# The planner's rate for gathers beside a dense expert stage: 380 in place of 360

## The chip, the cores and the metric

The kernel runs on one core of a Trainium2 chip. The metric is device time in microseconds, the median of several executions. The profile is of one execution.

## The reference

The reference is one residual block on 1024 tokens of width 1024 in float32. Three token mixers (stick-breaking attention, dilated window attention, attention into 256 memory tokens) share one normalised input, are gated, summed and projected, and added to x. Then comes the part that matters here, an expert mixer. Each token gets 8 heads x 16 = 128 of 16384 experts, each expert being one row of u and one of v:

```
act = gelu(einsum('chkd,cd->chk', u[ic], hc))     # ic: 128 chosen experts per token
w   = gate * act
out = einsum('chk,chkd->cd', w, v[ic])
```

## The kernel before, in words

The 1024 tokens are eight tiles of 128. The front (mixers, gating, output projection, and the choice of the experts) takes the tiles in three groups of 2, 3 and 3. The expert mixer is done in two ways.

**By gather**, for six tiles (0, 1, 2, 3, 5, 7). A tile takes 128 steps (class `Experts`, `step`, L1133). A step covers one expert for each of 128 token-head slots: GpSimd gathers 128 rows of u and later 128 rows of v with an indirect DMA each (`fetch`, L1097). VectorE multiplies the u rows with the spread tokens `hb` and sums them (L1151). After each fourth step ScalarE and VectorE make gelu and weights, and TensorE adds the v rows of those four steps into `po` (L1177, eight matmul instructions per step in the profile). There are `UP, VP = 5, 6` buffers for u and v rows. Every 32 steps a quarter of the output rows is loaded (`row`, L1142), added to and stored.

**Densely**, for the tiles 4 and 6 (`DENSE`, ND = 2), by `dense()`: all 16384 experts, in 128 blocks e of 128. A block has a product of u with the tokens (`product`, L1297 to L1305: 24 matmuls of 256 columns with high and low parts `uh`, `ul`, `hh`, `hl`), a gelu, a weighting by the gate matrix `g` (`weigh`, L1337), and 12 matmuls of 512 columns that sum into the output (`wh`, `wl` by `vh`, `vl`). The weights `ur` and `vr` come in pairs of blocks, 1 MB a load, through SP's queue (`load`, L247), with two buffers each; a `g` load of 1 MB serves eight blocks. ScalarE and VectorE split each weight block into high and low parts (L128, L1275). Before that the last tile's gate matrix is built (L1316: 80 fills) and stored to `gd`, and 22 blocks (`RUN`) get an early product at full precision. The products of the other 106 blocks follow, each with the sums of the block that is 22 earlier; the last 22 blocks have sums alone.

The order of the two is set when the program is built, by a planner (L1424 on). It keeps two sums: `pe`, the planned time of TensorE, and `dma`, that of the transfers, and places one gather step after another. Ahead of each it takes dense or front work from a generator in small pieces (`fill`, L1412), for as long as planned DMA is ahead of planned TensorE or TensorE is behind `due`:

```
L1416    spent = (cost[0] - c + 50) * slow[0], (moved[0] - m) / bw[0]
...
L1428    due = max(due + LEAST, pe - LEAST)
L1429    while filler[0] is not None and (dma > pe or pe < due):
L1430        a, b = fill(1)
L1431        pe += a
L1432        dma += b
L1433    pe += TOKEN_NS
L1434    dma += TOKEN_BYTES / bw[0]
```

Costs come from the code itself: a matmul through `mm` costs 4 x (columns/2.4 + 2.5) ns, one through `mmr` columns/2.4 + 3 ns, a gate fill 800 ns, and each fill 50 ns on top. `load` counts its bytes (L245). `slow` and `bw` have two values each: 1.38 and 295 bytes per ns during the front, and from L1405, where the front is closed and `dense()` begins, `SLOW[1]` = 1.1 and `BW[1]`. A step counts `TOKEN_NS` = 700 ns and `TOKEN_BYTES` = 128 x 8192 + 3 x 8192 = 1,073,152 bytes; `LEAST` is 3000 ns. When the generator has run out, the gather steps that are left follow alone.

Of the kernel before, what the change touches and what calls it, by code (L numbers as in the profile page):

```python
# [34 lines left out]
RUN = 22  # L35


BW = 295.0, 360.0
SLOW = 1.38, 1.1
TOKEN_NS, TOKEN_BYTES = 700.0, 128 * 8192 + 3 * 8192.0  # L40
LEAST = 3000.0
# [36 lines left out]
def block_kernel(ctx: ExitStack, tc: tile.TileContext, io):  # L78
# [1309 lines left out]
    def rest():  # L1388
        n0 = built = 0
        odd = False  # L1390
        for g in range(len(GROUPS)):
            for stage in phase1(g, n0, GROUPS[g], ready):
                if stage and built < ND:

                    want = sum(n < n0 for n in DENSE)
                    while len(stored) < want:
                        sides(1)
                    odd = not odd
                    for _ in range(999 if stage == 2 else 1 + odd):
                        if built < want:  # L1400
                            built = next(gates)
                yield
            n0 += GROUPS[g]
        front.close()
        slow[0], bw[0] = SLOW[1], BW[1]  # L1405
        yield from dense()

    filler = [rest()]
    slow, bw = [SLOW[0]], [BW[0]]
    pe = dma = due = 0.0  # L1410
# [86 lines left out]
```

## Time and profile before

| | us |
|---|---|
| median of 3 runs | 3561.07 |
| lowest and highest run | 3557.21, 3573.94 |
| the profiled execution, its own time | 3568.14 |
| its span, first to last instruction | 3566.4 |
| PE, DVE, POOL, ACT busy | 3196.1, 2341.1, 1778.4, 1353.6 |
| mean DMA rate over the span | 332 GB/s |

PE is TensorE's matmuls, PEld its weight loads, DVE is VectorE, ACT ScalarE, POOL GpSimd, SP the queue of SyncE that issues most loads. In the windows view each row is a stretch of the span; for each engine it has the busy microseconds and, in brackets, the number of instructions, then the granted TensorE clock, the mean busy share of the 16 DMA engines, and the rate. With a tile's name the busy times are of the instructions on that tile alone, but clock, share and rate are still those of the whole core. Rows of the waits view have who waited, for whom, the total in us, the number of times and the longest. Rows of a tile's view have minimum, median and maximum duration in ns and the first and last start in us.

### The profile page before, as it was taken

What the parts mean: (1) busy time and instruction counts of PE and PEld (TensorE: products, weight loads), DVE (VectorE), ACT (ScalarE), POOL (GpSimd) and SP (SyncE); (2) the same over time, 40 slices, a digit from 0 to 9 for tenths busy, and PEclk for the clock granted to TensorE, in tenths of its full rate; (3) what the DMA queues carried; (4) which work ended last, traced back from release to release, by engine and by line L of the source; (5) the groups of instructions that cost most, each with busy time, mean ns of one, the idle gap of its engine ahead of it and who ended that gap; (6) DMA issues with size and microseconds to landing.
All of it is one profiled execution on the core that took longest, in us unless ns stands there. A gap on an engine that the chain in (4) does not pass through costs nothing.

```text
span 3566.4 us, 60764 instructions
## 1 busy us (share of the span) xinstructions
PE 3196.1 (90%) x22802; PEld 2361.1 (66%) x22802; DVE 2341.1 (66%) x5985; ACT 1353.6 (38%) x2729; POOL 1778.4 (50%) x1544
## 2 busy tenths in 40 slices
PE   6999989989999889999998999776779999999954
PEld 6889856656555766666565657654568888888710
DVE  5444487565545468996656665798867677777654
ACT  4443135554411214656544222222324444444410
POOL 0000036656566556666555655566745444544476
PEclk9989989999999999999999999897899999999965
DMA  4425669999899999999998999989999999999999
GB/s 151 139 84 182 206 221 334 333 348 331 313 406 392 403 363 347 337 331 350 331 355 296 391 391 400 350 325 348 393 386 393 365 382 384 394 379 372 344 383 362
DMA packets 346430, 1185.54 MB, mean 332 GB/s; under 512 B 38744, under 2 KB 80216, under 8 KB 326680
## 3 DMA queue, kind: packets, MB, share of 16 engines
q0 software_dynamic: 221184, 805.40, 59.6%
q1 hardware_dynamic: 102672, 337.95, 26.0%
q10 hardware_dynamic: 22280, 38.31, 2.8%
q8 instruction: 180, 2.95, 0.3%
q14 instruction: 114, 0.93, 0.1%
HBM read 1142.18 MB, written 39.32 MB: 331 GB/s over the span
## 4 chain that ended last, share of the span: by engine, by line
PE 61%; DMA 15%; DVE 13%; issue 5%; ACT 3%; POOL 2%; ACTq 0%; SPq 0%; POOLq 0%; DVEq 0%
PE bank L117 32%; PE bank L1195 20%; PE po L1177 7%; DMA u<-in_u,iT 7%; DVE u L1151 3%; DMA v<-in_v,iT 3%; PE pb L1090 1%; DMA b3d<-sp 1%; PE bank L121 1%; POOL v L1097 1%; POOL u L1097 1%; DMA g<-gd 1%; ACT L126 1%; DMA gd<-g 1%; ACT e L128 1%
## 5 line engine op out<-in xcount | busy, mean ns | idle before, releaser
L1097 POOL DMA_INDIRECT u<-in_u,iT x768 | 916.2, 1193 | 956.1 <-DVE i L865 489.6
L1097 POOL DMA_INDIRECT v<-in_v,iT x768 | 861.4, 1122 | 818.8 <-PE po L1177 646.0
L1151 DVE SCALAR_TENSOR_TENSOR u<-u,hb 128x1024 f32<-128x1024 f32 x768 | 926.7, 1222 | 440.1 <-ACT hb L128 256.3
L1177 PE MATMUL po<-v,wz 128*32 128x256 f32 x6144 | 444.8, 416 | 155.3 <-DMA v<-in_v,iT 88.6
L117 PE MATMUL bank<-wide,w 128*128 128x384 f32 x1536 | 519.6, 492 | 1.8 <-DMA w<-in_w_gate 1.8
L1177 PEld LDWEIGHTS po<-v,wz 128*32 128x32 f32 x6144 | 182.0, 115 | 375.0 <-DMA v<-in_v,iT 119.0
L117 PEld LDWEIGHTS bank<-wide,w 128*128 128x128 f32 x1536 | 292.3, 192 | 201.3 <-issue 6.8
L128 ACT ACTIVATE hb<-pb 128x512 f32<-128x512 f32 x384 | 208.2, 594 | 397.2 <-PE pb L1090 251.3
L117 PEld LDWEIGHTS bank<-w,wide 128*128 128x128 f32 x2304 | 263.0, 192 | 7.4 <-issue 2.2
L117 PE MATMUL bank<-w,wide 128*128 128x128 f32 x2304 | 265.3, 275 | 0.2 <-DMA w<-in_w_out 0.2
L1195 PE MATMUL bank<-hh,ul 128*128 128x256 f32 x848 | 240.0, 283 | 1.2 <-DVE ul L1275 1.2
L1195 PE MATMUL bank<-hh,uh 128*128 128x256 f32 x848 | 240.9, 284 | 0.0
L1195 PE MATMUL bank<-hl,uh 128*128 128x256 f32 x848 | 239.9, 283 | 0.0
L117 PE MATMUL bank<-big,w 128*128 128x256 f32 (+1 forms) x1280 | 235.6, 341 | 1.2 <-DMA w<-in_w_pq 1.2
L117 PEld LDWEIGHTS bank<-big,w 128*128 128x128 f32 x1280 | 208.3, 193 | 27.0 <-issue 3.0
L128 ACT ACTIVATE e<-bank 128x512 f32<-128x512 f32 (+2 forms) x208 | 109.6, 527 | 306.8 <-PE bank L117 301.2
L1195 PE MATMUL bank<-vh,wh 128*128 128x512 f32 x512 | 202.9, 403 | 3.1 <-ACT vh L128 3.1
L1195 PE MATMUL bank<-vl,wh 128*128 128x512 f32 x512 | 201.9, 394 | 2.1 <-DVE vl L1275 2.0
L1195 PE MATMUL bank<-vh,wl 128*128 128x512 f32 x512 | 199.4, 389 | 0.0
L126 ACT ACT_TABLE_LOAD x144 | 184.8, 1283 | 21.7 <-issue 8.8
L128 ACT ACTIVATE w<-bank 128x256 f32<-128x256 f32 x128 | 49.3, 385 | 366.9 <-PE bank L1195 285.5
L1275 DVE TENSOR_TENSOR vl<-vr,vh 128x1024 fp32r<-128x1024 f32 x128 | 156.9, 1226 | 32.7 <-ACT vh L128 32.7
(297 smaller groups left out, 5659.9 us busy)
## 6 DMA issues: line engine op xcount, KB each, us to landing
ur<-in_uT SPq DMA_DIRECT2D x64, 1024.0 KB
vr<-in_vd SPq DMA_DIRECT2D x64, 1024.0 KB
w<-in_w_in SPq DMA_DIRECT2D x102, 512.0 KB
w<-in_w_gate SPq DMA_DIRECT2D x72, 512.0 KB
w<-in_w_pq SPq DMA_DIRECT2D x48, 512.0 KB
g<-gd SPq DMA_DIRECT2D x16, 1024.0 KB
w<-in_w_o SPq DMA_DIRECT2D x48, 256.0 KB
w<-in_w_out SPq DMA_DIRECT2D x24, 512.0 KB
```

The lines of the kernel that those rows point to most:

```text
L117: nc.tensor.matmul(out, lhsT, rhs, **kw)
L121: nc.tensor.transpose(out, in_, ident)
L126: nc.scalar.preload_act_table_set(s)
L128: nc.scalar.activation(out, in_, f, **kw)
L1090: nc.tensor.matmul(pb, which[:, jj].rearrange("p q s -> p (q s)"), box["b3"][:, f], start=True, stop=True)
L1097: nc.gpsimd.indirect_dma_start(out=t, out_offset=None, in_=io[kind], in_offset=bass.IndirectOffsetOnAxis(ap=ap, axis=0))
L1151: nc.vector.scalar_tensor_tensor(u, u, 1.0, self.hb, op0=OP.mult, op1=OP.mult, accum_out=self.parts[:, i:i + 1])
L1177: nc.tensor.matmul(po[32 * k:32 * k + 32, h:h + 256], wz[:, i, :], v[:, 256 * k:256 * k + 256], start=jj == 0 and i == 0, stop=jj == QB - ...
L1195: nc.tensor.matmul(out, lhsT, rhs, **kw)
L1275: nc.vector.tensor_sub(lo, r[:, x], hi)
```

## The change

One constant of the planner changes, the second of the two rates. It is used in L1405 alone, and from there in L1416 and L1434.

```
-BW = 295.0, 360.0
+BW = 295.0, 380.0
 SLOW = 1.38, 1.1
 TOKEN_NS, TOKEN_BYTES = 700.0, 128 * 8192 + 3 * 8192.0
 LEAST = 3000.0
```

No instruction is added or taken away. The order in which dense pieces and gather steps are issued can differ from the place where the front is closed.

More of the change, by code (lines that the diff above doesn't have):

```diff
@@ L35 @@
 RUN = 22
-BW = 295.0, 360.0
+BW = 295.0, 380.0
 SLOW = 1.38, 1.1
```

## The prediction

> **What bounds the kernel now.** I read the page first, then windows cut at the stage borders, the waits of each stage, and the chain that ended last.
>
> ```profile
> span 3566.4 us, 60764 instructions
> DMA  4425669999899999999998999989999999999999
> GB/s 151 139 84 182 206 221 334 333 348 331 313 406 392 403 363 347 337 331 350 331 355 296 391 391 400 350 325 348 393 386 393 365 382 384 394 379 372 344 383 362
> q0 software_dynamic: 221184, 805.40, 59.6%
> L1097 POOL DMA_INDIRECT u<-in_u,iT x768 | 916.2, 1193 | 956.1 <-DVE i L865 489.6
> L1097 POOL DMA_INDIRECT v<-in_v,iT x768 | 861.4, 1122 | 818.8 <-PE po L1177 646.0
> ur<-in_uT SPq DMA_DIRECT2D x64, 1024.0 KB
> vr<-in_vd SPq DMA_DIRECT2D x64, 1024.0 KB
> g<-gd SPq DMA_DIRECT2D x16, 1024.0 KB
> ```
>
> The page gives the sizes. The 1536 gathers moved 805.4 MB, 0.524 MB each, so a gather step (one u, one v) moves 1.049 MB. The rate of 360 acts only once the front is closed, so only the end of the span can change. It has four stages, whose borders are the first and last product (hl,uh) and the last sum (vh,wl):
>
> ```profile
> L1195 PE MATMUL bank<-hl,uh x848: 279/283/283, 2653.3 to 3320.8; 128*128 128x256 f32 x170
> L1195 PE MATMUL bank<-vh,wl x512: 387/389/402, 2656.4 to 3400.7; 128*128 128x512 f32 x171
> ```
>
> ```profile
> core 0: us, PE busy (x) PEld busy (x) DVE busy (x) ACT busy (x) POOL busy (x), PEclk, DMA share, GB/s
> 2380.00:2653.30 273.30, 184.39 (x1250) 125.78 (x1250) 222.40 (x727) 72.10 (x216) 162.64 (x135) 0.83 0.95 362
> 2653.30:3320.80 667.50, 666.99 (x4895) 575.13 (x4895) 478.41 (x741) 309.90 (x514) 319.11 (x244) 1.00 0.99 380
> 3320.80:3400.70 79.90, 75.27 (x415) 54.91 (x413) 54.62 (x87) 34.06 (x56) 38.27 (x32) 1.00 0.90 336
> 3400.70:3566.40 165.70, 78.35 (x542) 16.24 (x540) 82.07 (x156) 17.59 (x46) 117.80 (x115) 0.54 0.97 380
> ```
>
> I call them prelude, body, end and tail. In the body PE is busy 666.99 of 667.50 us while DMA also shows a share of 0.99. The waits say which of the two is the limit. These are the body's only waits for DMA; then the two largest of SP's queue there; then the tail's three largest for DMA:
>
> ```profile
> DVE u L1151 <- DMA u<-in_u,iT: 2.9, 1, 2.9
> POOL v L1097 <- DMA u<-in_u,iT: 0.3, 1, 0.3
> ```
>
> ```profile
> SPq L247 <- DVE ul L1275: 212.7, 40, 8.8
> SPq L247 <- DVE vl L1275: 202.9, 48, 7.3
> ```
>
> ```profile
> PEld po L1177 <- DMA v<-in_v,iT: 90.9, 41, 3.3
> PE po L1177 <- DMA v<-in_v,iT: 66.9, 50, 2.4
> DVE u L1151 <- DMA u<-in_u,iT: 65.1, 51, 4.5
> ```
>
> In the body nobody waits for data (2.9 us in 667.5), and the dense loads wait for a free buffer, not for DMA. PE sets the pace. In the tail it is the reverse: PE and DVE wait for each gather. So work on DMA that leaves the tail and fits beside the body's matmuls is gained, less what it costs PE there.
>
> **How many steps move.** The planner adds 0.7 us of planned time and 1,073,152 bytes per step, and fills with dense work while planned DMA is ahead. Over a stage with P us of planned dense work and D bytes of dense transfers it therefore places n = (P - D/rate) / (1,073,152/rate - 0.7) steps. The divisor is 2.281 us at 360 and 2.124 us at 380.
>
> One product of the body is 24 matmuls of 109.7 ns, 12 of 216.3 ns and three fills of 50 ns, times 1.1: 5.916 us; its bytes are 1.049 MB of weights and an eighth of a g load, 1.180 MB. That gives 1.157 steps at 360 and 1.324 at 380, so for 106 products 122.6 and 140.3: 17 to 18 more. The prelude has 14 waiting fills (22.4 us), 80 gate fills (68.0 and, for 64 of them, two matmuls, 28.6), 22 early products (76.9) and 0.3 for six fills: 196.1 times 1.1 is 215.7 us. Its bytes are 24 MB-sized transfers (13 ur, 8 stores to gd, the tokens, one vr, one g), 25.2 MB. n goes from 63.9 to 70.4, 7 more. The end has 46 pieces of six sums (1.348 us each, times 1.1: 68.2 us) and 12 such transfers, 12.6 MB; it goes from 14.6 to 16.5, 2 more. I take 7, 17 and 2: 26 steps leave the tail. The trace bears out the formula at 360, eight po matmuls to a step:
>
> ```profile
> 2653.30:3320.80 667.50, 58.66 (x968) 28.28 (x968) 1.68 (x4) 1.00 0.99 380
> 3320.80:3400.70 79.90, 7.74 (x128) 3.75 (x128) 0.42 (x1) 1.00 0.90 336
> ```
>
> ```profile
> 3400.70:3566.40 165.70, 0.00 (x0) 0.00 (x0) 73.88 (x120) 0.00 (x0) 56.53 (x55) 0.54 0.97 380
> ```
>
> The body has 968/8 = 121 steps, the end 16. The last row is of tile u, with two DVE records to a step: 60 steps lie in the tail, so 34 would be left.
>
> **The tail, minus 67.6 us.** Two price rows, the tail's undisturbed stretch and a short full stretch of the body:
>
> ```profile
> 2640.00:2700.00 60.00, 58.84 (x382) 49.55 (x381) 44.49 (x77) 25.77 (x44) 26.16 (x21) 0.96 1.03 398
> 3420.00:3480.00 60.00, 28.70 (x192) 5.27 (x192) 30.58 (x56) 4.92 (x13) 45.99 (x47) 0.50 1.03 409
> ```
>
> At 409 GB/s a step takes 2.56 us; the whole tail, with its lead-in and drain, 165.7/60 = 2.76. Lead-in and drain stay, so I take 2.6, near the first: 26 x 2.6 = 67.6, bounds 66.6 and 71.8.
>
> **The body, plus 21.** What a step costs PE is seen in the chain, where four steps' po matmuls lie between two dense pieces:
>
> ```profile
> 3100.94 22.48 PE bank L1195 x144
> 3123.43 1.86 PE po L1177 x32
> 3125.83 21.09 PE bank L1195 x138
> ```
>
> From 3123.43 to 3125.83 are 2.40 us, 0.60 per step. 17 steps add 10.2 us: by PE the body is 677.7 us. By DMA it has 667.5 x 380 GB/s = 253.7 MB and 17.8 MB more, 271.5 MB: 664 us at 409, 682 at 398, 714 at 380. So both limits come out nearly equal, and where they do each sometimes waits for the other. The cover is the dense loads' second buffer and eleven gather buffers; if it is gone, PE waits for ul or vl behind a late load. I take 688.5, 10.8 over the PE bound, which asks for 394 GB/s, near the 398 of the full stretch. Bounds: +10 and +47 (380 GB/s is all there is).
>
> **The prelude, plus 13.** Its last 210 us are nearly full already:
>
> ```profile
> 2440.00:2520.00 80.00, 67.53 (x467) 49.77 (x468) 64.13 (x235) 25.53 (x84) 51.79 (x41) 0.94 0.99 384
> 2520.00:2610.00 90.00, 69.96 (x451) 47.27 (x451) 80.96 (x267) 25.32 (x90) 60.25 (x51) 0.89 1.00 391
> ```
>
> Seven steps bring 7.3 MB. Beside the 210 x 388 = 81.5 MB there they end 6 us later if DMA reaches 409, 19 later at 388. I take 13, between.
>
> **The end, plus 2.** Here PE is idle for 79.90 less 75.27, 4.6 us, into which two steps of 0.60 fit. Against it stands 2 x 2.6 = 5.2 if each delays a load by its own transfer. Bounds 0 and 5; I take 2.
>
> A count may also shift by one step per stage. POOL's queue is passed by 26 pairs of gathers earlier than before; it is busy 319 of 667.5 us in the body. SP's queue gets the row loads (L1142, four per 32 steps) of 26 steps sooner, three or four of them, with dense loads queued behind; the second buffer covers those. Nothing is added or removed in bytes, matmuls or splits.
>
> Sum: 13 + 21 + 2 - 67.6 = -31.6 us. The span goes from 3566.4 to 3534.8, the profiled execution's own 3568.1 to 3536.5. That execution lies 7 us above the median of the runs, 3561.1, from which the forecast is 3529.5.
>
> **The rivals.** Full gain: the body takes its steps at PE's price. For it: nobody waits for data now. 6 + 10 + 0 - 71.8 = -56, 3505. Chance 0.17.
>
> No change, because DMA is already at its limit: each step costs in the body what it cost in the tail. For it: the share of 0.99 and the 380 GB/s of both body and tail. Against: 398 and 409 in shorter stretches. 47 + 19 + 5 - 67.6 = +3, 3564. With what lies between, 0.22. The Trainium skill has a rule for this side: "DMA: Bandwidth & Descriptors", Specifications, sets the HBM limit per core at about 358 GB/s. By it a plan at 380 asks for what can't be had: the 27.3 MB of the 26 steps would take 76 us where they go, against 68 saved, +8 in all by this estimate. This case's trace disagrees: the body's 380 and the tail's 409 lie above that limit. "HBM Reference", Specifications (TRN2), says that a core streaming alone measures about 425, which these rows come nearer to.
>
> Slower: with the queues full, a dense load lands after its use, PE stalls at ul or vl, buffers come free late, SP's next load is issued late, and DMA idles, as in the end, where DMA fell to 336 GB/s:
>
> ```profile
> ACT vh L128 <- DMA vr<-in_vd: 5.9, 2, 3.0
> ```
>
> At 358, midway between 380 and 336, the body takes 758 us, +91, and the sum is 91 + 19 + 5 - 67.6 = +47, 3608. It makes the kernel slower by over 0.5% only from a body of 730 us, below 372 GB/s. Against it: 11 gathers stay in flight whether PE stalls or not. 0.06.
>
> No effect: the planner's other condition, 3.0 us of planned time per step, sets the count. Against: in the body a step comes every 667.5/121 = 5.5 us. 0.02, at 3561.
>
> **How the numbers follow.** The forecast's chance is 0.53. What a measurement can tell from no change is about 0.5%, 17.8 us. Forecast and full gain are faster by more (0.70); no change and no effect lie within (0.24); 0.06 is slower. The range goes from just under the full gain, 3502, to 3558, near no change: above it are the slower case and part of the no-change case, below it almost nothing.
>
> **What would show it.** In the profile after, the first product comes at about 2666 instead of 2653, and the body from first to last product takes about 688 us with some 138 steps. The tail has 34 steps (68 records on u) and is near 98 us. The body's GB/s rises to about 394, with short waits for ul, vl or u new in it. The forecast is wrong if the body's rate stays near 380 and the body grows by 40 us or more, or if the tail still holds 60 steps.

## The result, and the profile after

The changed kernel takes 3549.23 us (median of 6 runs, 3540.80 to 3550.15), the kernel before, beside it, 3571.22 (6 runs, 3557.21 to 3574.48). The ratio is 0.9942, 95% interval 0.9921 to 0.9963: 0.58% faster, where the forecast was 0.9% (31.6 of 3568.1 us). Run once more on another chip, the ratio was 0.9931 (0.9908 to 0.9954). The profiled execution after has its own time of 3549.34 us and a span of 3547.6, that is 18.8 us less than the span before, not 31.6.

The page after:

```profile
span 3547.6 us, 60760 instructions
DMA  4425669899899999999998999998999999999999
GB/s 152 140 86 179 208 219 344 329 347 327 313 406 401 405 367 337 336 339 342 343 342 283 388 400 399 348 341 332 361 380 383 405 393 396 401 396 406 372 352 369
```

The DMA digits say the same as before, 9 almost everywhere, but in the 32nd to 37th slice, all body, the rate is 393 to 406, where it was 365 to 394. Next the rows that give the stage borders, then the windows cut there (PE, PEld, DVE, ACT, POOL busy, then clock, DMA share, GB/s), then the same windows for tile po, and the tail for tile u:

```profile
L1195 PE MATMUL bank<-hl,uh x848: 278/283/415, 2680.0 to 3367.2; 128*128 128x256 f32 x170
L1195 PE MATMUL bank<-vh,wl x512: 387/389/632, 2684.5 to 3450.0; 128*128 128x512 f32 x171
```

```profile
2380.00:2680.00 300.00, 195.79 (x1294) 129.12 (x1293) 234.08 (x745) 73.93 (x218) 169.14 (x148) 0.81 0.94 355
2680.00:3367.20 687.20, 681.68 (x5052) 582.32 (x5052) 495.08 (x779) 315.06 (x527) 357.64 (x278) 0.99 1.01 394
3367.20:3450.00 82.80, 77.40 (x415) 55.95 (x413) 56.40 (x92) 35.12 (x58) 42.68 (x35) 0.98 0.94 357
3450.00:3547.60 97.60, 47.77 (x338) 10.19 (x336) 46.98 (x90) 9.74 (x25) 65.64 (x64) 0.53 0.93 365
```

```profile
2680.00:3367.20 687.20, 67.69 (x1120) 32.81 (x1120) 2.11 (x5) 0.99 1.01 394
3367.20:3450.00 82.80, 7.74 (x128) 3.75 (x128) 0.00 (x0) 0.98 0.94 357
```

```profile
3450.00:3547.60 97.60, 0.00 (x0) 0.00 (x0) 40.64 (x66) 0.00 (x0) 31.27 (x30) 0.53 0.93 365
```

The body has 1120/8 = 140 steps instead of 121, the end 16 as before, the tail 66/2 = 33 instead of 60. Set against the forecast, stage by stage:

| stage | before, us | after, us | change | forecast (bounds) |
|---|---|---|---|---|
| prelude, to the first product | 273.3 | 300.0 | +26.7 | +13 (6 to 19) |
| body | 667.5 | 687.2 | +19.7 | +21 (10 to 47) |
| end | 79.9 | 82.8 | +2.9 | +2 (0 to 5) |
| tail | 165.7 | 97.6 | -68.1 | -67.6 |

Three of the four terms came within 1.3 us, and together 0.9 us below their sum. The prelude took 13.7 us more than its term and 7.7 more than its upper bound; that is the miss of 12.8. In the body there are now waits for transfers and split weights that were absent or shorter before (DVE's for u was 2.9), each of them short, as said. Four of the largest:

```profile
DVE u L1151 <- DMA u<-in_u,iT: 27.0, 13, 3.2
ACT vh L128 <- DMA vr<-in_vd: 7.4, 3, 3.7
PEld bank L1195 <- DVE vl L1275: 6.6, 5, 3.1
PE bank L1195 <- DVE vl L1275: 5.0, 3, 2.8
```

### The profile page after: what moved, and what is told of

The parts are those of the page before. It is cut to its first block, busy times and chain, and to the rows that moved or that the text cites. A ratio compares the mean times of both kernels' runs of the same rounds, so it can differ in the third digit from the quotient of the medians.

```text
span 3547.6 us, 60760 instructions
## 1 busy us (share of the span) xinstructions
PE 3194.0 (90%) x22802; PEld 2366.4 (67%) x22802; DVE 2337.2 (66%) x5985; ACT 1354.3 (38%) x2729; POOL 1768.6 (50%) x1544
## 4 chain that ended last, share of the span: by engine, by line
PE 60%; DMA 15%; DVE 14%; issue 5%; ACT 4%; POOL 2%; ACTq 1%; SPq 0%; POOLq 0%; DVEq 0%
PE bank L117 33%; PE bank L1195 17%; PE po L1177 7%; DMA u<-in_u,iT 5%; DVE u L1151 4%; DMA v<-in_v,iT 3%; DMA b3d<-sp 2%; PE pb L1090 1%; PE bank L121 1%; DMA gd<-g 1%; DMA vr<-in_vd 1%; POOL v L1097 1%; POOL u L1097 1%; ACT L126 1%; DMA ur<-in_uT 1%
## 5 line engine op out<-in xcount | busy, mean ns | idle before, releaser
L1097 POOL DMA_INDIRECT v<-in_v,iT x768 | 842.4, 1097 | 764.1 <-PE po L1177 595.1
L1177 PE MATMUL po<-v,wz 128*32 128x256 f32 x6144 | 434.8, 411 | 112.1 <-DVE wz L1166 54.3
L1195 PE MATMUL bank<-hh,ul 128*128 128x256 f32 x848 | 240.8, 284 | 0.4 <-DVE ul L1275 0.4
```

The lines of the kernel that those rows point to most:

```text
L1097: nc.gpsimd.indirect_dma_start(out=t, out_offset=None, in_=io[kind], in_offset=bass.IndirectOffsetOnAxis(ap=ap, axis=0))
L1177: nc.tensor.matmul(po[32 * k:32 * k + 32, h:h + 256], wz[:, i, :], v[:, 256 * k:256 * k + 256], start=jj == 0 and i == 0, stop=jj == QB - ...
L1195: nc.tensor.matmul(out, lhsT, rhs, **kw)
```

## The experiments

Two questions are open. Is the tail's gain real when the prelude is left alone, and how far does it go? And why did the prelude cost 26.7 us? Nearly all kernels change only the planner's rate, by stage: X from the close of the front (the prelude), Y from the first product on (body and end):

```
-BW = 295.0, 360.0
+BW = 295.0, X
...
         behind[0], wait[0] = True, False
+        bw[0] = Y
```

In the table, "build" is the part of the prelude in which the work of the planned rate lies: from the first load of the split tokens (vr<-h2d, at 2428.3 us before) to the first product (2653.3 before). It leaves out what the front's end adds by chance. "Planned" is the number of steps that the planner puts in the prelude. The last column has what all DMA queues of the core moved in the build and the mean rate.

| run | X, Y | ratio (95%) | planned | build | body | end | tail | build: MB, GB/s |
|---|---|---|---|---|---|---|---|---|
| before | 360, 360 | 1 | 64 | 225.0 | 667.5 | 79.9 | 165.7 | 87.2, 387 |
| after | 380, 380 | 0.9942 (0.9921-0.9963) | 71 | 251.5 | 687.2 | 82.8 | 97.6 | 95.5, 380 |
| e1 | 360, 380 | 0.9911 (0.9890-0.9931) | 64 | 230.3 | 677.9 | 86.7 | 113.3 | 87.2, 379 |
| e2 | 380, 360 | 1.0034 (1.0020-1.0048) | 71 | 247.2 | 666.2 | 85.5 | 148.9 | 94.9, 384 |
| e3 | 360, 400 | 0.9889 (0.9872-0.9905) | 64 | 225.1 | 723.7 | 83.9 | 60.3 | 87.2, 388 |
| e4 | 360, 420 | 0.9861 (0.9842-0.9880) | 64 | 226.0 | 763.7 | 100.3 | 5.5 | 87.9, 389 |
| e8 | 360, 440 | 0.9928 (0.9915-0.9941) | 64 | 227.5 | 811.7 | 72.9 | 5.0 | 88.3, 388 |
| e12 | 360, 410 | 0.9877 (0.9861-0.9892) | 64 | 223.1 | 741.7 | 91.0 | 34.5 | 87.5, 392 |
| e7 | 300, 420 | 0.9891 (0.9875-0.9907) | 46 | 192.4 | 767.2 | 85.1 | 56.8 | 69.0, 359 |
| e11 | 350, 420 | 0.9848 (0.9832-0.9864) | 61 | 216.4 | 762.3 | 87.5 | 17.5 | 83.9, 388 |
| e10 | 370, 420 | 0.9888 (0.9872-0.9905) | 68 | 233.1 | 764.3 | 91.3 | 5.5 | 90.2, 387 |
| e9 | 375, 420 | 0.9885 (0.9868-0.9903) | 69 | 238.1 | 773.5 | 84.9 | 5.0 | 91.3, 384 |
| e17 | 377, 377 | 0.9948 (0.9929-0.9966) | 70 | 235.1 | 683.5 | 84.0 | 110.5 | 91.2, 388 |
| e18 | 380, 380 | 0.9931 (0.9908-0.9954) | 71 | 249.4 | 686.6 | 83.1 | 98.2 | 94.6, 379 |
| e13 | 377, 420 | 0.9831 (0.9806-0.9855) | 70 | 237.0 | 772.0 | 85.6 | 5.0 | 91.6, 387 |
| e14 | 380, 420 | 0.9904 (0.9883-0.9924) | 71 | 258.5 | 764.2 | 85.4 | 5.0 | 94.9, 367 |
| e15 | 390, 420 | 0.9898 (0.9878-0.9919) | 74 | 245.3 | 779.1 | 85.8 | 5.0 | 94.6, 385 |
| e16 | 335, 420 | 0.9901 (0.9881-0.9920) | 57 | 222.8 | 762.6 | 95.4 | 30.1 | 80.0, 359 |

The last four ran on a chip where the kernel before took 3711.46 us and the tokens were loaded 114 to 138 us later; they are compared only with each other, and by the lengths. The other runs were made on several chips where the kernel before took 3567 to 3571 us.

The lengths are of one profile each. How far profiles differ where the prelude has the same plan is seen in the six kernels with X = 360: their builds take 223.1 to 230.3 us at 379 to 392 GB/s.

**The two stages apart: e1 (X 360, Y 380) and e2 (X 380, Y 360).**

> Rate 360 in the prelude, 380 from the first product on. By the planner's sum the prelude has 64 steps as before, the body 139, the end 20, the tail 40. Theory 'chain' (the prelude is a chain of gate copies and gd stores, so that a step put there costs about 3.8 us, more than the 2.6 us that it saves in the tail): prelude back at 273 us, body 687, end 83, tail about 113, span 3536, some 30 us below the kernel before and 11 below the change. Rival 'bytes' (a step costs its transfer, 2.6 us, wherever it is, and the rest of the prelude's 26.7 us is chance of this order): 7 steps are 18 us more in the tail and 18 less in the prelude, no difference from the change, about 20 us below the kernel before.

> Rate 380 in the prelude, 360 from the first product on: 71, 121, 18 and 53 steps. Theory 'chain': prelude 300 us, body 667, end 80, tail about 147: some 8 us slower than the kernel before. Rival 'bytes': within 3 us of the kernel before.

e1 took 3537.39 us against 3567.22 before, e2 3578.47: 30 us less and 11 more, near the numbers of "chain" and not those of "bytes" (that "chain" has the wrong reason is seen further on). So the change consists of a gain from the rate of the body and a loss from that of the prelude. Not all of e2's loss lies in the prelude itself: its end is 5.6 us longer than before, with the same 16 po steps. With the prelude left alone the kernel is 0.9% faster, the amount that was forecast for the whole; with the prelude alone it is 0.3% slower. The body of e1:

```profile
2653.30:3331.20 677.90, 677.62 (x5030) 581.02 (x5030) 498.55 (x784) 314.69 (x526) 359.36 (x278) 1.00 1.02 402
```

PE is busy 677.62 of 677.90 us: it is the PE bound of the prediction (677.7), at 402 GB/s, which the prediction had put into the rival "full gain". By rate and length it moves 272.5 MB there. The changed kernel's body moves 270.8 MB, no more, and takes 9 us longer. Of these, 1.8 are three more po steps at 0.60, and 5 are idle time of PE (5.5 us against 0.3). A limit of DMA at 394 GB/s did not force that; where it comes from was not tried.

**How far the body goes: e3 (400), e4 (420), e8 (440), e12 (410), all with X 360.**

> Rate 360 in the prelude, 400 from the first product on: 64, 158, 21 and 20 steps. The body then moves 292.5 MB. If DMA can give 409 GB/s there, the body takes about 718 us and the span is about 3517; if 394 GB/s, what the change reached, is the ceiling, the body takes 742 us and the span is about 3541, so that the 19 steps more give nothing beyond the rate of 380.

> Rate 360 in the prelude, 420 from the first product on: 64 steps, 176, and all of the rest in the end, no tail. The body moves 311 MB. At 409 GB/s it takes 761 us and the span is about 3514; at 394 GB/s 790 us and 3543. If the full queues make PE wait for ul and vl so that DMA goes idle as well, the body is longer than 790 us and the kernel is slower than with 400.

> Rate 360 in the prelude, 440 from the first product on: 64 steps, 196 in the body, 3 in the end, no tail. The body moves 332 MB. If 404 GB/s, what the runs at 400 and 420 reached, is the ceiling, it takes 823 us, the end has sums alone, about 75 us, and the span is about 3551: slower by some 26 us than with 420. If DMA can still go to 416 GB/s, body 799 us, span 3527, as with 420.

> Rate 360, then 410: between the two fastest so far (400: 3528, 420: 3519). Some 10 steps are left for the tail. The prelude is as before (273 to 276 us), the body about 742 us, the tail 30 to 35 us: 3519 to 3527. If the turning point lies below 420, it is faster than 420; the sum of the stage prices (0.6 to 2.3 us for a step in the body beside 2.5 in the tail) says it is within 5 us of it.

They took 3527.85, 3518.97, 3542.49 and 3527.35 us. The bodies of e4 and e8:

```profile
2655.90:3419.60 763.70, 724.57 (x5336) 603.25 (x5336) 541.07 (x875) 325.62 (x554) 423.18 (x347) 0.97 1.02 404
```

```profile
2659.30:3471.00 811.70, 748.88 (x5507) 610.30 (x5507) 566.75 (x926) 331.49 (x569) 470.07 (x386) 0.95 1.02 406
```

Between 402 (e1) and 406 GB/s (e8) nothing more was to be had: past this a step costs the body nearly its transfer (1.049 MB at 406 GB/s are 2.6 us). By the po records, e3's body has 20 steps more than e1's for 45.8 us (2.3 each); e8's 20 more than e4's for 48.0 (2.4), and PE's idle time grows from 0.3 us to 39 and 63. The tail pays 2.65 per step (113.3 less 60.3, for 20), so up to 420 there should be a little to win. The median at 420 is 9 us below that at 400, but the intervals overlap and the two profiled spans say the opposite (3525.4 and 3520.6), so it is not shown. At 440 nearly all steps lie in the body, the end has 8 and its rate falls to 177 GB/s, and the kernel is slower than at 420. 410, on another chip, can't be told from 400 or 420.

**Whether the stores of the gate blocks hold the prelude up: e5 (380) and e6 (360), one rate for all stages.** In the profile after, ScalarE waits in the prelude longer for the stores of the gate matrix than before, when it was 26.1 us and 5.7 the longest:

```profile
ACT g L128 <- DMA gd<-g: 36.7, 6, 9.6
```

Here every second quarter of the gate matrix (32 tokens) uses a second pair of buffers, lying in the room of `hh` and `hl`. Half of the gate values are rounded by that to the type of these two tiles, fp32r, so the output is a little less exact.

```
-                sg = [room() for _ in range(2)]
+                sg = twins if twins and tb % 2 == 0 else [room() for _ in range(2)]
...
         hl = dp.tile([128, KD, TD], F32R, name="hl", bufs=1)
+        twins.extend(x.rearrange("p k t -> p (k t)").rearrange("p (i t) -> p i t", t=32) for x in (hh, hl))
```

> The change (380 throughout), and the gate matrix has two pairs of buffers ahead of its stores in place of one: every second quarter is built in the room of hh and hl, which are free until then. (Half of the gate values are rounded to 12 bits or so on the way, so the output is a little less exact; no work is left out.) In the change ScalarE waited 36.7 us in the prelude for gd stores to land, in the kernel before 26.1. Theory 'stores' (those waits carry what the seven steps cost too much): prelude from 300 down to about 275 us, the kernel some 25 us faster than the change. Rival 'other work' (DVE's selection and the row output hold the prelude as well, and the wait for the stores lies beside them): prelude within 8 us of 300.

> The same two pairs of gate buffers in the kernel before (360 throughout; half of the gate values rounded). Theory 'stores': prelude from 273 to about 255 us, and the difference to the run at 380 with the same buffers falls from 27 us to the price of seven transfers, about 18. Rival 'other work': prelude 265 or more, and the difference stays near 27.

e5 took 3537.37 us, ratio 0.9915 (0.9900 to 0.9929), which is not 25 us below the change, and e6 3564.29, 0.9992 (0.9981 to 1.0003). The waits for the stores are gone in both. What DMA moved in the builds, first before and after, then e6 and e5:

```profile
DMA packets 24471, 87.17 MB, mean 387 GB/s; under 512 B 2488, under 2 KB 7051, under 8 KB 21723
DMA packets 26755, 95.50 MB, mean 380 GB/s; under 512 B 2741, under 2 KB 7330, under 8 KB 23936
```

```profile
DMA packets 24633, 87.81 MB, mean 397 GB/s; under 512 B 2503, under 2 KB 7076, under 8 KB 21868
DMA packets 26708, 95.25 MB, mean 396 GB/s; under 512 B 2736, under 2 KB 7324, under 8 KB 23909
```

With the second pair the rate is 396 to 397 GB/s, and the build takes 240.8 us at 380 and 221.3 at 360, 19.5 apart. That is the seven steps' own transfer: the 7.4 MB more take 19 us at 396. The two kernels without the second pair lie 26.5 apart. Of these, 8.3 MB more at the 387 GB/s of before are 21.5 us, and the rest, some 5, is the lower rate of 380. So the stores are not the main cause; they may have a share of up to 7 us, but builds of one plan differ by as much. "Stores" had the difference right for the builds (some 18); "other work" had the length of the prelude right (268 us in e6).

**What a step costs in the prelude: e7 (300), e9 (375), e10 (370), e11 (350), all with Y 420.** The three of 350 to 375 also test a second theory. In the compiled program SP's queue has at 360 and 375 a g load and a ur load in turn; at 350, 370 and 380 two g loads stand together ahead of the last ur loads.

> Rate 300 in the prelude (46 steps in place of 64), 420 from the first product on (176 in the body, 24 in the end, 17 in the tail). If a step costs 3.8 us in the prelude on this side of 360 too, the prelude falls by 68 us to 205 and the kernel gains about 21 us on the run with 360 and 420 (17 steps, some 47 us, come back in the tail). If it costs 2.6 us, 226 us and no difference. If the prelude is held by its own chain with few gathers, about 250 us, and the kernel is some 25 us slower than with 360 and 420.

> Rate 375 from the close of the front, 420 from the first product on. Open is why the last stretch of the prelude, from the last store of gate blocks to the first product, grew from 42 to 52 us at 380. In the compiled order SP's queue has at 375 the same order there as at 360 (a g load, then a ur load, in turn), while at 380 two g loads stand together in front of the last ur loads. The planner places 69 steps in the prelude here, 64 at 360, 71 at 380. Theory 'queue order': the last stretch is 41 to 44 us as at 360, and the prelude about 285 us (48 to the load of the tokens, 180 + 5 x 2.5 for the stretch of the gate blocks, 43, and 2). Theory 'steps': the stretch goes with the steps in it and is 48 to 52 us, the prelude about 294 us. Time against 360/420 (3519): 'queue order' +10, less what the 5 steps relieve at the end; 'steps' +15 to +20.

> Rate 370, then 420: one step fewer in the prelude than at 375, but here the compiled order of SP's queue has two g loads together ahead of the last ur loads, as at 380. 'Queue order': last stretch 50 to 54 us, prelude about 291 us, so it is slower than 375/420 by some 6 us although it has a step less there. 'Steps': last stretch and prelude at most those of 375/420.

> Rate 350, then 420: 61 steps planned in the prelude, three fewer than at 360, but SP's queue has the two g loads together, as at 380. 'Queue order': the last stretch is about 50 us where 360/420 had 41, the prelude about 275 us, as long as with 360 or longer, and the time is 3525 to 3530, slower than 360/420. 'Steps': the last stretch is 38 to 41 us, the prelude about 267 us, and the time within 5 us of 360/420's 3519.

They took 3530.34, 3531.33, 3530.19 and 3516.28 us. By the builds, 18 planned steps from 300 to 360 cost 33.6 us (226.0 of e4 less 192.4; 1.9 each), and the five from 360 to 375 12.1 (2.4 each). So the 3.8 us a step of "chain" fell. At 300 the build's rate is only 359 GB/s; from 350 to 377 it is 379 to 392, and there a step's transfer alone is 2.7 us. The tail pays 2.65 per step, and at 360 no tail is left, so by these totals the prelude is at its best near 350 to 360: with fewer steps there (e7) they go to the tail, which then lasts 56.8 us. "Queue order" missed in the total: 350 and 370 have the two g loads together and lie on the line of the step price. It hit one part: from the last gate store to the first product 350 takes 49.1 us where 360 took 44.8, which its earlier part gives back (167.3 us against 181.2). For 370 and 375 it missed that stretch too: 46.1 and 48.3 us, the other way round than it said.

**Is 380 a jump? e13 (377), e14 (380), e15 (390), e16 (335), Y 420.** Between 375 and 380, two planned steps, the build rose from 238 to 247 and more.

> Rate 377, then 420: the planner places 70 steps in the prelude (69 at 375, 71 at 380), and the compiled order of SP's queue is the one of 360 and 375 in its g and last ur loads. 'Jump by order': the prelude is about 288 us, one step's 2.5 us above 375's 285.4, and the time is near 375/420's 3531. 'Rising price': it is 290 to 295 us, midway between 375 and 380, and the time 3535 to 3540.

> Rate 380, then 420: the changed kernel's prelude with the body of 420. Both theories: prelude 297 to 300 us, as in the three kernels at 380. 'Jump by order': the time is 10 us above 377/420. 'Rising price': 3 to 6 us above it.

> Rate 390, then 420: 74 steps in the prelude, three more than at 380, with the order of SP's queue that 370 has. 'Jump by order': the jump of 380 is gone, and the prelude is 370's 282.9 and 6 steps of 2.5, about 298 us, no longer than at 380. 'Rising price': 310 us or more.

> Rate 335, then 420: 57 steps in the prelude, four fewer than at 350. By the price between 300 and 350 (25.7 us for 15 steps, 1.7 each) the prelude is about 260 us, and the four steps go to the tail at some 2.5 us each: 3517 to 3523, a little slower than 350/420. If the price near 350 is already above 2.5 us, it is faster, 3510 to 3515.

The builds are 237.0, 258.5, 245.3 us and, at 335, 222.8. So 390, with three steps more than 380, is 13.2 us shorter, and 377, with one less, 21.5 shorter. A price that rises with the steps does not fit that. The last column says what differs: 390 and 380 move nearly the same (94.6 and 94.9 MB), but 380 does it at 367 GB/s and 390 at 385. 377 moves 3.3 MB less. The totals (3647.42, 3676.63, 3676.49, 3679.24) say less: of the 36 us between the profiled spans of e13 and e14, 18 lie ahead of 2084 us (the first store of the other dense tile's gate blocks comes at 2084.1 and 2101.8 us), where the two programs are the same. On the best prelude rate e16 is inconclusive: its build moves only 80.0 MB, at 359 GB/s, and is as long as that of 360 elsewhere.

**The change and its neighbour on one chip: e17 (377) and e18 (380, the change again), one rate for all stages.**

> One rate of 377 for prelude, body and end, as the change has 380: planned 70, 136 and 19 steps against 71, 139 and 19, so 38 are left for the tail and not 34. 'Jump by order': from the load of the tokens to the first product it takes 232 to 236 us (375/420: 234.4, 377/420: 233.1), the change 244 to 256; the prelude's 10 to 15 us less outweigh the four steps more in the tail (10 us, less 4 us in body and end), so it is 4 to 9 us faster than the change. 'Price of the steps': the stretch is one step shorter than the change's, 2.5 to 4 us, and the kernel 2 to 4 us slower than the change.

> The changed kernel once more, beside the one at 377 on the same chip. Both theories: ratio near 0.994, 244 to 256 us from the load of the tokens to the first product.

e17 took 3545.38 us, e18 3540.24, and the intervals of the ratios overlap. The build behaves as "jump by order" said, 235.1 and 249.4 us. The 4 to 9 us in the total do not show; the medians stand the other way round. In the two profiled spans (3542.6 and 3540.8) e17 is 4 us shorter from the load of the tokens on, and that load came 6 us later. What the longer build costs lies below what the totals resolve. In its build the change moves 3.4 MB more than 377 here (4.3 in the first profile of it), which at 388 GB/s are 9 to 11 of the 14.3 to 16.4 us; the rest is its lower rate, 379 to 380.

One difference between the two can be seen in SP's queue, in order of time (start, duration). First the change (after), then 377 (e17):

```profile
2627.62 0.33 SPq L247 DMA_DIRECT2D ur<-in_uT  x1
2633.98 5.71 SPq L247 DMA_DIRECT2D g<-gd  x2
2639.78 7.22 SPq L247 DMA_DIRECT2D ur<-in_uT  x1
2658.75 0.36 SPq L247 DMA_DIRECT2D g<-gd  x1
2659.21 0.52 SPq L247 DMA_DIRECT2D ur<-in_uT  x1
```

```profile
2615.63 0.33 SPq L247 DMA_DIRECT2D ur<-in_uT  x1
2626.20 0.38 SPq L247 DMA_DIRECT2D g<-gd  x1
2626.68 0.89 SPq L247 DMA_DIRECT2D ur<-in_uT  x1
2629.89 0.38 SPq L247 DMA_DIRECT2D g<-gd  x1
2636.33 5.30 SPq L247 DMA_DIRECT2D ur<-in_uT  x1
2647.94 13.56 SPq L247 DMA_DIRECT2D g<-gd  x2
```

And the chain that ended last, of the change, in the same place:

```profile
2625.44 8.46 DMA gd<-g
2633.98 17.21 DMA g<-gd
...
2657.38 1.35 DVE w L1341 x4
2658.75 0.36 SPq L247
2659.21 16.70 DMA ur<-in_uT
2675.94 1.06 ACT uh L128
...
2678.30 11.76 PE bank L1195 x62
```

In the change the third g load stands ahead of the ur load of blocks 22 and 23, the first two products. It needs a g buffer, which VectorE's weighting of the first eight blocks (L1341) sets free at 2658.7; only then is the ur load issued, at 2659.2, and its landing at 2675.9 starts the products. At 377 the same ur load goes out at 2636.3, ahead of the third g load. By this chain it accounts for the last stretch: from the last gate store (2625.9 and 2617.0) to the first product are 54.1 us against 47.6. In all four profiles with X = 380 and one pair of buffers this stretch takes 54.1 to 55.9 us, at 377 and 390, where the ur load stands ahead of the third g load, 47.6 to 48.5. But the order alone does not make the build long. The traces show the order of 380 at 300, 335 and 350 too, and 350 keeps 388 GB/s over its build. The larger part of the difference, 9.9 of 16.4 us, lies before the last store (197.4 us against 187.5). That part takes 195.1 and 191.3 us in e18 and e2, and 196.8 at 390, so it is not peculiar to 380. The order was not tried by itself.

## Why the prediction was right in its direction and wrong in its size

**The body, right, but in part by luck.** It took +19.7 us for 19 po steps, at 394 GB/s, as said. The PE price held: 19 steps at 0.60 are 11.4 us, and by itself (e1) the body keeps to PE. The other 8.3 us match the allowance of 10.8 for two limits that "come out nearly equal", and waits for vl behind late loads came as described. But DMA was not at its limit there: e1 moved as many bytes at 402 GB/s nearly without those waits.

**The end and the tail, right.** +2.9 and -68.1 us; 27 steps left the tail, at 2.52 us each.

**The prelude, wrong.** The step that failed is "I take 13, between", with its bounds 6 and 19: the term of the sum measured +26.7, 26.5 of it in the build. The count and the bytes were right: 64 u and 63 v gathers are issued in the build where 57 and 56 were, seven steps, or 7.3 MB. Wrong was what DMA would do with them. 13 us mean that the last 210 us and 13 more move 81.5 + 7.3 MB, a rate of 398 GB/s where 388 was measured; the bound of 6 (7 by its own figures) takes the tail's 409. The rate did not rise with the demand. It was 387 in the build before, 379 to 384 in the three profiles of this plan on the faster chips, and at most 392 in any kernel with one pair of gate buffers. Seven steps at 387 are 19 us, the upper bound. The rest of the 26.5 us is about 1 MB of other transfers (2 to 3 us), which a later first product also lets through, and the fall from 387 to 380 GB/s (some 5 us), which is within what builds of one plan differ. With the second pair of buffers, where the rate is 396 in both builds, the steps cost 19.5.

Why the build at 377 has only 4 MB more than before for six more planned steps, and at 380 again 3 to 4 MB more for one, is open. A place in SP's queue is part of it: the prediction costed that queue at "the second buffer covers those", for row loads alone, while by the chain the ur load of the first product stood behind a g load that waited for its buffer. This is argued for 6.5 of the 16.4 us between 377 and the change, and not tried.

The working also has a small slip that changes nothing: 14 waiting fills of 1.55 us, by the kernel's costs, are 21.7 and not 22.4, a third of a step.

**The rivals.** "No change, because DMA is already at its limit" fell: the body's rate rose to 394 and, by e1 to e8, to 406. The Trainium skill's rule in "DMA: Bandwidth & Descriptors", Specifications, about 358 GB/s per core, does not hold here: the bodies moved 379 to 406. The Trainium skill's figure of about 425 in "HBM Reference", Specifications (TRN2), was not reached over a stage; 402 to 406 was the highest beside the dense stage. "Full gain" held for the body of e1 (+10.4 us, where it had 10), but in the change the body took 19.7 and the prelude 26.7, where it had 6. The slower case, body below 372 GB/s, did not come, and came at no rate up to 440. "No effect" fell with the count: 140 steps in the body where 121 were.

**The number.** The forecast started from the 3561.07 us of three runs; six runs gave 3571.22. So 10 of the 20 us between 3529.5 and 3549.23 are the starting point, and the rest is the prelude's excess (13.7 us in the profiled pair, whose gain is 3 us below that of the medians). The result lies within the range, and barely beyond the 0.5% that was called telling.

**A better kernel.** With a rate for each stage, 350 and 420, the median is 3516.28 us, ratio 0.9848 (0.9832 to 0.9864), against the change's 0.9942. 360 and 420 (0.9861), on another chip, can't be told from it.

## What to carry to other kernels

A rate that a planner uses for several stages is several changes at once: price the step in each stage (here 0.6 us beside PE-bound work, 1.9 to 2.8 in the prelude, 2.5 to 2.65 in the tail) and set it by stage. Price bytes that are added to a stage whose DMA is already busy at the rate of that stage, not at a higher one seen in another stage (387 here, not 409), unless a run shows that it rises. What waits in a queue behind a load that has no buffer yet is worth a look as well (6 to 8 us in one stretch here, by the chain). Find a DMA limit by raising the demand until the stage grows by about the transfer's own time, not by the busy share.

## What the runs showed of the hardware

The busy share of the DMA engines did not tell how much was left. It was 0.99 in the body before, at 380 GB/s, and 1.01 to 1.02 at 394 to 406. In the build it was 1.00 at 387 GB/s, and 1.01 at 396 to 397 with the second pair of gate buffers. A single core moved 402 to 406 GB/s over 680 to 810 us beside a PE that was busy 92 to 100% of the time.

The chips differ: of those used here, one took 3711 us for the kernel before where the others took 3567 to 3571. In the four kernels profiled on it the tokens were loaded 114 to 138 us later than before, and the bodies had 403 to 404 GB/s, as the others at 420 (403 to 406).
